# Where the pre-added weight tiles of a two-layer trunk are loaded from, and when they are rounded

## The chip, the cores and the metric

The kernel runs on one core of a Trainium2 chip. The metric is the device time of one execution in microseconds (us); lower is better. Three runs of the kernel before took 2234.64, 2239.62 and 2239.37 us, so its median is 2239.37 us.

## The reference, cut to what matters

The program computes two layers of a trunk on 256 tokens of width 2048, in fp32. Each layer has two halves:

```
h = rms_norm(x, pre_mix_norm);  mix = two kinds of attention over h @ w_in
x = x + rms_norm(mix @ w_o, post_mix_norm)
h = rms_norm(x, pre_ffn_norm)
x = x + rms_norm((silu(h @ w_gate) * (h @ w_up)) @ w_down, post_ffn_norm)
```

`w_gate` and `w_up` are 2048 x 5632, `w_down` is 5632 x 2048. All weights are read once. The change touches the second half of a layer alone: the gate and up products with the `silu` between them, called the gate stage here, and the product with `w_down`, called the down stage.

## The kernel before, in words

**Products.** TensorE (PE) works in fp32r. To keep fp32 accuracy each operand is split into a rounded part `hi` (or `jh`, `sh`, `Th`) and the rest `lo` (`jl`, `sl`, `Tl`), and one product becomes three matmuls: hi*hi, hi*lo, lo*hi (`product`, L730). Each matmul has 128 x 128 weights loaded and 512 columns streamed.

**Weights.** All weights lie in DRAM in the order of use, as 784 tiles of 128 x 1024 floats (512 KB). `fetch` (L149) issues the loads: a tile goes into one of four `raw` buffers by a DMA on SyncE's queue (SP, L159). `feed` (L195) splits a loaded tile: ScalarE (ACT) rounds it into `hi` (L205), and VectorE (DVE) subtracts to get `lo` (L207). There are six `hi` and six `lo` buffers. A product asks for its tile and for the four that follow (`LOOKAHEAD`).

**Gate stage.** It runs over eleven chunks of 512 columns (L854). In each chunk eight pairs `kp` of 128-row blocks are summed; a pair has one tile of `w_gate` and one of `w_up`. Both halves of the tokens meet both tiles, so an ordinary pair is eight products of 128 x 128 x 512, 24 matmuls (`eight`, L837). For some pairs the 2 x 2 block product is done with seven products instead, 21 matmuls (`seven`, L847, and `seven_products`, L750). These pairs, called sevens here, are listed in `SEVEN` (in chunk 0 in `FIRST_SEVEN`), those of the down stage in `DOWN_SEVEN`; there a pair is two neighbouring column tiles of `w_down`, summed over 22 pairs, once for each half of the columns.

**Sums for a seven.** It needs sums of weight blocks. One of them is made by the DMA engines: `summed` (L164) loads the up tile into a buffer `T` by a plain DMA on SP (L167), and a second DMA, on GpSimd's queue (POOL, L168), adds the first half of the gate tile onto it. The second must wait until the first has landed. There are three `T` buffers in the gate stage and two in the down stage. `summed` is called `EARLY` tiles ahead of the fetch. The rest is done by `mixed_weights` (L172): ACT rounds `T` and DVE subtracts (L181, L182), DVE makes three more sums (L186 to L188), overwriting the gate tile in its `raw` buffer, and two more roundings and differences give `Th` and `Tl`, first of 512 columns from `T`, then of 1024 from `raw`, called the last rounding and the last difference here. The token side needs sums too: `pair_sums` and `token_sums` (L830, L737) make them on DVE once a layer for each pair in `SEVEN`; in chunk 0 this is spread by `FORM_AT`, which says ahead of which step which pair's sums are made.

**End of a chunk.** Four banks `p1`, `p6`, `p7`, `q5` that the sevens share are folded into the results (`shared_part`, L767), then DVE adds the four results, ACT applies Silu, and DVE multiplies (L878 to L883). The activations are transposed on PE and copied by ACT into `act` (`flip`, L885). `flip` is started with a delay of `DEFER_ACT` ticks; a tick (`tick`) is counted once every six matmuls or so as products are emitted, so `DEFER_ACT` = 5 puts the transposes in the second pair of the following chunk.

**Order.** A planner orders the instructions of each engine when the program is built, from their priorities and its own estimate of when their inputs are ready; `issue_after` forbids it to put an instruction ahead of a named one. On the chip each engine and each DMA queue runs its instructions strictly in that order, and one that waits holds up all behind it.

Of the kernel before, what the change touches and what calls it, by code (L numbers as in the profile page):

```python
# [2 lines left out]

# [9 lines left out]
AF = mybir.ActivationFunctionType  # L13
# [11 lines left out]
FF = 5632  # L25
CW = 512
# [2 lines left out]
LOOKAHEAD = 4  # L29
PACE = 2  # L30
DEFER = 8
DEFER_ACT = 5
URGENT = 50
TAIL = 3
KP_O = (4, 5, 6, 7, 0, 1, 2, 3)
SEVEN = (2, 4, 5, 6)
FIRST_SEVEN = (4, 6)
FIRST_ORDER = (0, 1, 3, 2, 4, 5, 6, 7)
FORM_AT = {1: 4, 3: 6, 4: 5, 5: 2}
DOWN_SEVEN = (2, 5, 8, 11, 14, 17)  # L40

WARM = 13
LEVEL = 232
EARLY = 4


def lambda_init(layer):
# [58 lines left out]
def kernel(  # L106
# [15 lines left out]
    nc = tc.nc  # L122
# [23 lines left out]
    raws, loads = [], []  # L146
# [15 lines left out]
    sums = {}  # L162

    def summed(i):  # L164

        sums[i] = mix_pool[0].tile([P, 2, CW], F32, tag="T", bufs=mix_pool[1], name=f"T{i}")
        loads.append(nc.sync.dma_start(sums[i], stream[i]))  # L167
        nc.gpsimd.dma_start(sums[i][:, 0, :], stream[i - 1][:, 0, :], accum_op=ALU.add)  # L168

    mix_pool = [None, 0, 0]  # L170

    def mixed_weights(i):  # L172

        g, u = raws[i - 1], raws[i]
        hi = wpool.tile([P, 2, CW], F32R, tag="hi", bufs=6, name=f"hi{i}")
        lo = wpool.tile([P, 2, CW], F32R, tag="lo", bufs=6, name=f"lo{i}")
        th = mix_pool[0].tile([P, 3, CW], F32R, tag="Th", bufs=2, name=f"Th{i}")
        tl = mix_pool[0].tile([P, 3, CW], F32R, tag="Tl", bufs=2, name=f"Tl{i}")

        def split(h, l, w):  # L180
            nc.scalar.activation(h, w, AF.Copy)  # L181
            nc.vector.tensor_tensor(out=l, in0=w, in1=h.bitcast(F32), op=ALU.subtract)  # L182

        split(hi, lo, u)
        t2 = u[:, 1, :]
        nc.vector.tensor_tensor(out=t2, in0=u[:, 0, :], in1=t2, op=ALU.add)  # L186
        nc.vector.tensor_tensor(out=g[:, 0, :], in0=t2, in1=g[:, 0, :], op=ALU.subtract)
        nc.vector.tensor_tensor(out=g[:, 1, :], in0=t2, in1=g[:, 1, :], op=ALU.add)  # L188
        split(th[:, 2, :], tl[:, 2, :], t2)
        split(th[:, 0:2, :], tl[:, 0:2, :], g)  # L190
        t1, b22 = ((hi[:, k, :], lo[:, k, :]) for k in range(2))
        t3, t4, t2 = ((th[:, k, :], tl[:, k, :]) for k in range(3))
        return {"b22": b22, "t1": t1, "t2": t2, "t3": t3, "t4": t4}

    def feed(upto):  # L195
        fetch(upto)
        while fed[0] < min(upto, len(stream)):
            i = fed[0]
# [3 lines left out]
                fed[0] += 1  # L202
                continue
            hi = wpool.tile([P, 2, CW], F32R, tag="hi", bufs=6, name=f"hi{i}")
            nc.scalar.activation(hi, raw, AF.Copy)  # L205
            lo = wpool.tile([P, 2, CW], F32R, tag="lo", bufs=6, name=f"lo{i}")
            nc.vector.tensor_tensor(out=lo, in0=raw, in1=hi.bitcast(F32), op=ALU.subtract)  # L207
            ready[i] = (hi, lo)
# [145 lines left out]
    def start(gen, n=1):  # L354
        running.append([clock[0] + n, gen])
# [421 lines left out]
    for l in range(L):  # L777
# [73 lines left out]
            a11, a12, a22 = (e[:, 0, 0:P], e[:, 1, 0:P]), (o[:, 0, 0:P], o[:, 1, 0:P]), (o[:, 0, P:S], o[:, 1, P:S])  # L851
            seven_products(banks, extra, forms[kp], a11, a12, a22, hi, lo, m, first, last)

        for c in range(FF // CW):  # L854
            banks = four_banks(c % 2, [f"c{q}_{l}_{c}" for q in ("11", "12", "21", "22")])
            mine = FIRST_SEVEN if c == 0 else SEVEN
            order = FIRST_ORDER if c == 0 else tuple(range(KT // 2))
# [21 lines left out]
            for t, u in ((0, w[1]), (1, w[3])):  # L879
                nc.vector.tensor_tensor(out=sg[t], in0=banks[2 * t], in1=sg[t], op=ALU.add)  # L880
                nc.scalar.activation(sg[t], sg[t], AF.Silu, scale=rs[t][:, 0:1])
                nc.vector.tensor_tensor(out=u, in0=banks[2 * t + 1], in1=u, op=ALU.add)
                nc.vector.scalar_tensor_tensor(out=sg[t], in0=u, scalar=rs[t][:, 0:1], in1=sg[t], op0=ALU.mult, op1=ALU.mult)  # L883

            def flip(sg=sg, at=at, c=c):  # L885
# [5 lines left out]
                    yield 1  # L891

            start(flip(), DEFER_ACT)
        gu.release()
        mix_pool[:] = new_x_pool(f"sums{l}"), 2, plan[l]["down"][3, FF // P // 2 - 1] + 1
        dn = tc.alloc_tile_pool(name=f"dn{l}", bufs=4, reuse_waits="tile")
# [146 lines left out]
```

## Time and profile before

| | us |
|---|---|
| median of 3 runs | 2239.37 |
| lowest and highest | 2234.64, 2239.62 |
| the profiled execution | 2239.96 |
| its span, first to last instruction | 2237.9 |
| busy in the span: PE, DVE, ACT, POOL | 2200.9, 1789.1, 1309.5, 132.0 |
| gate stage, layer 0 and layer 1, about | 412 to 882, 1526 to 1996 |

A row of the profile names the engine, the line of the kernel and the tiles as out<-in. "SPq" is the queue of SyncE, and the DMAs of L168 stand under POOL. PE's matmuls overlap: each is shown with about 0.39 us, but the next starts 0.23 us after it, so PE can be shown as busy while it is waiting, and starts are to be compared, not durations. DVE's steps overlap a little in the same way.

### The profile page before, as it was taken

To read this page: it belongs to the slowest core of one execution; us is meant where nothing else is said; L and a number is where in the kernel's file an instruction comes from. 1 tells how busy PE (TensorE), PEld (TensorE's weight loads), DVE (VectorE), ACT (ScalarE), POOL (GpSimd) and SP (SyncE) were. 2 spreads that over 40 slices of the span, in tenths; PEclk is the share of its full clock that TensorE was granted. 3 is DMA by queue.
4 is the path that set the end of the run, shared out by engine and by line. 5 is a ranking of instruction groups with operands and counts; after the bars stand their busy time and mean duration, and the time that the engine had idled before them with its cause. 6 is when DMAs were issued, how large, how long until landed. Compare 5 with 4: busy or idle time off the path is not lost.

```text
span 2237.9 us, 28440 instructions
## 1 busy us (share of the span) xinstructions
PE 2200.9 (98%) x10057; PEld 1802.2 (81%) x10057; DVE 1789.1 (80%) x2531; ACT 1309.5 (59%) x1937; POOL 132.0 (6%) x184
## 2 busy tenths in 40 slices
PE   9999999999999999999999999999999999999998
PEld 7888888777887888788878888887777887878886
DVE  6666555899988999989776665558999999998897
ACT  6545554665655656656565455546665566566664
POOL 1100000000000000000010000000000000000000
PEclk9999999999999999999999999999999999999999
DMA  8555455576776676766555544556677677666673
GB/s 290 189 167 164 160 190 183 186 223 209 226 242 199 212 251 190 228 214 205 193 184 171 168 162 160 188 186 192 206 218 237 218 222 234 221 203 222 203 232 132
DMA packets 133326, 452.05 MB, mean 202 GB/s; under 512 B 15296, under 2 KB 15808, under 8 KB 132672
## 3 DMA queue, kind: packets, MB, share of 16 engines
q1 hardware_dynamic: 117488, 421.91, 55.2%
q0 software_dynamic: 15552, 28.32, 7.6%
q8 instruction: 79, 1.29, 0.2%
q14 instruction: 63, 0.52, 0.1%
q10 hardware_dynamic: 144, 0.02, 0.0%
HBM read 448.09 MB, written 2.10 MB: 201 GB/s over the span
## 4 chain that ended last, share of the span: by engine, by line
PE 71%; DVE 13%; DMA 6%; issue 4%; ACT 4%; POOL 0%; DVEq 0%; ACTq 0%; SPq 0%; POOLq 0%
PE in L380 7%; PE in L382 7%; PE in L381 7%; DMA raw<-in_weights_in_turn_dram 5%; PE c L733 5%; PE c L734 5%; PE c L735 5%; PE dn L938 5%; PE dn L936 5%; PE dn L935 4%; DVE lo L207 3%; DVE Tl L182 2%; PE o L382 2%; PE o L381 2%; PE o L380 2%
## 5 line engine op out<-in xcount | busy, mean ns | idle before, releaser
L207 DVE TENSOR_TENSOR lo<-raw,hi 128x1024 fp32r<-128x1024 f32 x675 | 824.1, 1225 | 311.4 <-ACT hi L205 307.3
L205 ACT ACTIVATE hi<-raw 128x1024 fp32r<-128x1024 f32 x675 | 709.4, 1057 | 510.9 <-DMA raw<-in_weights_in_turn_dram 178.4
L733 PE MATMUL c<-hi,xF 128*128 128x512 f32 x820 | 321.0, 395 | 2.4 <-DVE w L774 1.3
L735 PE MATMUL c<-hi,xF 128*128 128x512 f32 x820 | 318.8, 391 | 0.0
L734 PE MATMUL c<-lo,xF 128*128 128x512 f32 x820 | 318.7, 389 | 0.0
L168 POOL DMA_DIRECT2D T<-in_weights_in_turn_dram x108 | 94.1, 871 | 1754.1 <-DMA T<-in_weights_in_turn_dram 821.8
L733 PEld LDWEIGHTS c<-hi,xF 128*128 128x128 f32 x820 | 154.0, 188 | 35.3 <-DVE w L774 2.5
L936 PE MATMUL dn<-lo,jh 128*128 128x512 f32 x464 | 180.8, 390 | 0.0
L935 PE MATMUL dn<-hi,jh 128*128 128x512 f32 x464 | 180.7, 389 | 0.0
L735 PEld LDWEIGHTS c<-hi,xF 128*128 128x128 f32 x820 | 153.9, 188 | 32.3
L734 PEld LDWEIGHTS c<-lo,xF 128*128 128x128 f32 x820 | 154.1, 188 | 30.9
L380 PE MATMUL in<-hi,xI 128*128 128x512 f32 x384 | 154.0, 401 | 0.2 <-ACT xI L321 0.2
L380 PE MATMUL in<-hi,xT 128*128 128x512 f32 x384 | 153.4, 400 | 0.2 <-ACT xT L616 0.2
L382 PE MATMUL in<-hi,xI 128*128 128x512 f32 x384 | 150.2, 391 | 0.3 <-DVE xI L326 0.3
L381 PE MATMUL in<-lo,xI 128*128 128x512 f32 x384 | 149.9, 390 | 0.5 <-DVE lo L207 0.5
L381 PE MATMUL in<-lo,xT 128*128 128x512 f32 x384 | 149.8, 390 | 0.5 <-DVE lo L207 0.5
L382 PE MATMUL in<-hi,xT 128*128 128x512 f32 x384 | 150.2, 391 | 0.0
L938 PE MATMUL dn<-hi,jl 128*128 128x512 f32 x464 | 143.3, 390 | 0.0
L182 DVE TENSOR_TENSOR Tl<-raw,Th 128x1024 fp32r<-128x1024 f32 x108 | 131.5, 1217 | 8.7 <-ACT Th L181 8.7
L181 ACT ACTIVATE Th<-raw 128x1024 fp32r<-128x1024 f32 x108 | 113.8, 1053 | 37.9 <-DVE raw L188 37.8
L182 DVE TENSOR_TENSOR lo<-T,hi 128x1024 fp32r<-128x1024 f32 x108 | 131.4, 1216 | 4.4 <-ACT hi L181 4.4
L181 ACT ACTIVATE Th<-T 128x512 fp32r<-128x512 f32 x108 | 67.9, 629 | 112.1 <-DVE T L186 96.3
(298 smaller groups left out, 4077.9 us busy)
## 6 DMA issues: line engine op xcount, KB each, us to landing
raw<-in_weights_in_turn_dram SPq DMA_DIRECT2D x675, 512.0 KB, 4.3
T<-in_weights_in_turn_dram SPq DMA_DIRECT2D x108, 512.0 KB, 4.4
T<-in_weights_in_turn_dram POOLq DMA_DIRECT2D x108, 256.0 KB, 6.5
xr<-in_x_columns_dram SPq DMA_DIRECT2D x8, 256.0 KB, 6.1
x<-in_x_dram SPq DMA_DIRECT2D x4, 512.0 KB, 9.2
gpost_mix<-in_post_mix_norm_dram SPq DMA_DIRECT2D x2, 1024.0 KB, 6.0
gpost_ffn<-in_post_ffn_norm_dram SPq DMA_DIRECT2D x2, 1024.0 KB, 8.1
out_dram<-x SPq DMA_DIRECT2D x8, 256.0 KB, 2.8
```

Source lines behind the costliest of these rows:

```text
L182: nc.vector.tensor_tensor(out=l, in0=w, in1=h.bitcast(F32), op=ALU.subtract)
L205: nc.scalar.activation(hi, raw, AF.Copy)
L207: nc.vector.tensor_tensor(out=lo, in0=raw, in1=hi.bitcast(F32), op=ALU.subtract)
L380: nc.tensor.matmul(a, sh, hi[:, kk, :], start=first and kk == 0, stop=False)
L381: nc.tensor.matmul(a, sh, lo[:, kk, :], start=False, stop=False)
L382: nc.tensor.matmul(a, sl, hi[:, kk, :], start=False, stop=last and kk == 1)
L733: nc.tensor.matmul(a, sh, hi, start=first, stop=False)
L734: nc.tensor.matmul(a, sh, lo, start=False, stop=False)
L735: nc.tensor.matmul(a, sl, hi, start=False, stop=last)
L935: nc.tensor.matmul(accs[c, t], sh, hi[:, kk, :], start=first, stop=False)
L936: nc.tensor.matmul(accs[c, t], sh, lo[:, kk, :], start=False, stop=False)
L938: nc.tensor.matmul(accs[c, t], sl, hi[:, kk, :], start=False, stop=last)
```

## The change

Six things are changed together.

- The plain load of `T` goes to GpSimd's queue, just ahead of the adding DMA of the same tile, and is no longer in the list `loads` that `load_gain` is ordered behind.
- `mixed_weights` notes its last rounding in `turns`; the rounding of an ordinary tile `i` may not be put ahead of the last rounding of any seven with `j <= i - 2` (`after_sums`).
- `DEFER_ACT` becomes 7, so the transposes come two ticks later.
- `EARLY` becomes 6.
- The sevens move: in the gate stage from pairs 2, 4, 5, 6 to 2, 3, 5, 6, in chunk 0 from 4, 6 to 5, 6, in the down stage from 2, 5, ... 17 to 3, 6, ... 18. Their number is the same, and so is the number of matmuls. `FORM_AT` follows.
- The two multiplications at the end of a chunk are written behind both pairs of sums. (The body of the loop over chunks becomes a function.)

```
-DEFER_ACT = 5
+DEFER_ACT = 7
...
-SEVEN = (2, 4, 5, 6)
-FIRST_SEVEN = (4, 6)
+SEVEN = (2, 3, 5, 6)
+FIRST_SEVEN = (5, 6)
 FIRST_ORDER = (0, 1, 3, 2, 4, 5, 6, 7)
-FORM_AT = {1: 4, 3: 6, 4: 5, 5: 2}
-DOWN_SEVEN = (2, 5, 8, 11, 14, 17)
+FORM_AT = {1: 5, 2: 6, 4: 2, 5: 3}
+DOWN_SEVEN = (3, 6, 9, 12, 15, 18)
...
-EARLY = 4
+EARLY = 6
...
         sums[i] = mix_pool[0].tile([P, 2, CW], F32, tag="T", bufs=mix_pool[1], name=f"T{i}")
-        loads.append(nc.sync.dma_start(sums[i], stream[i]))
+        nc.gpsimd.dma_start(sums[i], stream[i])
         nc.gpsimd.dma_start(sums[i][:, 0, :], stream[i - 1][:, 0, :], accum_op=ALU.add)
...
+    turns = []
+
+    def after_sums(i):
+
+        done = [ins for j, ins in turns if j <= i - 2]
+        return tc.issue_after(done[-1]) if done else nullcontext()
...
         def split(h, l, w):
-            nc.scalar.activation(h, w, AF.Copy)
+            rounded = nc.scalar.activation(h, w, AF.Copy)
             nc.vector.tensor_tensor(out=l, in0=w, in1=h.bitcast(F32), op=ALU.subtract)
+            return rounded
...
-        split(th[:, 0:2, :], tl[:, 0:2, :], g)
+        turns.append((i, split(th[:, 0:2, :], tl[:, 0:2, :], g).ins))
...
-            nc.scalar.activation(hi, raw, AF.Copy)
+            with after_sums(i):
+                nc.scalar.activation(hi, raw, AF.Copy)
...
                 nc.vector.tensor_tensor(out=u, in0=banks[2 * t + 1], in1=u, op=ALU.add)
+            for t, u in ((0, w[1]), (1, w[3])):
                 nc.vector.scalar_tensor_tensor(out=sg[t], in0=u, scalar=rs[t][:, 0:1], in1=sg[t], op0=ALU.mult, op1=ALU.mult)
```

More of the change, by code (lines that the diff above doesn't have):

```diff
@@ L1 @@
 import math
-from contextlib import ExitStack
+from contextlib import ExitStack, nullcontext
 import concourse.bass as bass
@@ L852, in seven, with chunk @@
             seven_products(banks, extra, forms[kp], a11, a12, a22, hi, lo, m, first, last)
-        for c in range(FF // CW):
+        def chunk(c):
             banks = four_banks(c % 2, [f"c{q}_{l}_{c}" for q in ("11", "12", "21", "22")])
@@ L893 @@
             start(flip(), DEFER_ACT)
+        for c in range(FF // CW):
+            chunk(c)
         gu.release()
```

## The prediction

> **What bounds the kernel now.** I read the page first, then who waited for whom on PE, then single chunks by time.
>
> ```profile
> PE 2200.9 (98%) x10057; PEld 1802.2 (81%) x10057; DVE 1789.1 (80%) x2531; ACT 1309.5 (59%) x1937; POOL 132.0 (6%) x184
> ```
>
> ```profile
> PE p L733 <- ACT Th L181: 6.5, 11, 1.5
> PE p L734 <- DVE Tl L182: 5.1, 9, 0.9
> PE p_d L733 <- ACT Th L181: 4.9, 2, 2.5
> ...
> PE actT_ps L889 <- DVE w L883: 2.1, 4, 0.9
> ```
>
> TensorE is the bound, and no matmul is added or removed, so only its pauses can be won. The second fence (us in total, times, longest) is most of them in the stages that the change touches: 6.5 + 5.1 + 4.9 + 2.1 = 18.6 us, most of it for the last sums of a seven. Each is counted from the modelled end of a matmul, so by starts a pause is a little longer. The starts of the first product with `Th` in pair 6 show how much:
>
> ```profile
> 529.12 0.39 PE L733 MATMUL p<-Th,sh 128*128 128x512 f32 x1
> ...
> 789.47 0.39 PE L733 MATMUL p<-Th,sh 128*128 128x512 f32 x1
> 831.26 0.39 PE L733 MATMUL p<-Th,sh 128*128 128x512 f32 x1
> 873.10 0.39 PE L733 MATMUL p<-Th,sh 128*128 128x512 f32 x1
> ...
> 1643.66 0.39 PE L733 MATMUL p<-Th,sh 128*128 128x512 f32 x1
> 1984.60 0.39 PE L733 MATMUL p<-Th,sh 128*128 128x512 f32 x1
> ```
>
> From 789.47 to 831.26 a chunk takes 41.79 us without a pause: 180 matmuls and 8 short transposes, 0.23 us a matmul. From chunk 2 (529.12) to chunk 10 (873.10) eight chunks take 343.98 us, 9.7 over 8 x 41.79 = 334.3; in layer 1, 340.94, 6.6 over. So 16.3 us are lost in these sixteen chunks. A part is not waiting but a slow clock:
>
> ```profile
> 789.47:831.26 41.79, 41.79 (x190) 34.50 (x188) 39.19 (x47) 25.30 (x29) 3.48 (x4) 1.00 0.73 229
> 704.95:708.36 3.41, 3.41 (x9) 2.65 (x8) 2.96 (x4) 0.34 (x1) 0.61 (x1) 0.50 1.08 333
> 899.51:902.92 3.41, 3.41 (x10) 2.64 (x9) 3.41 (x5) 2.41 (x3) 0.00 (x0) 0.50 0.89 281
> ```
>
> In these windows the granted clock (third number from the end) falls to 0.50 for 3.41 us, right behind the longest pauses of layer 0 (1.5 and 0.9 above, and 2.35 below), which costs 1.7 us each time. The Trainium skill, "TensorE: Matmul & The Clock Gate", "What's actually happening", says that TensorE drops to half clock after an idle window of about 3.4 us. The trace is stricter: shorter pauses did it here.
>
> The first row also shows DVE (the fourth number with a bracket is ACT, the third DVE) busy for 39.19 of 41.79 us. It has 2.6 us of play in a chunk, and its order decides when the last sums of a seven are there:
>
> ```profile
> 825.45 0.68 DVE L186 TENSOR_TENSOR T<-T 128x512 f32<-128x512 f32 x1
> 826.05 1.22 DVE L207 TENSOR_TENSOR lo<-raw,hi 128x1024 fp32r<-128x1024 f32 x1
> ...
> 829.00 1.21 DVE L207 TENSOR_TENSOR lo<-raw,hi 128x1024 fp32r<-128x1024 f32 x1
> 830.13 1.22 DVE L182 TENSOR_TENSOR Tl<-raw,Th 128x1024 fp32r<-128x1024 f32 x1
> ```
>
> Steps follow each other after 0.60 us (512 columns) or 1.14 us (1024). The last difference of pair 6 ends at 831.35. The product that uses it is the one after 831.26, so it starts at 831.49: 0.14 us of margin in a chunk without a pause. Any DMA that is late breaks it, as in this piece of the chain that ended last, where PE was waiting:
>
> ```profile
> 694.57 6.25 DMA raw<-in_weights_in_turn_dram
> ...
> 703.14 1.23 DVE Tl L182
> ```
>
> An ordinary load takes 6.25 us; its rounding stands ahead of the last rounding of pair 6 on ACT, so that the difference that PE needs comes at 703.14.
>
> **The change, part by part.** *Ordering roundings behind the sums.* In the old order the two differences shown at 826.05 and 829.00, of tiles for pair 7 and the next chunk, stand ahead of the last difference of pair 6. In the new order they stand behind it, and so do their roundings on ACT. That takes 2 x 1.14 = 2.3 us off its time: the margin goes from 0.14 to about 2.4 us. What is pushed back is late next: the difference of the first up tile of the following chunk. PE takes this one only after pair 7 (24 matmuls), so it is covered; uncovered it would cost its 1.14.
>
> *Sevens at 2, 3, 5, 6.* Three in a row become two and two, so a late seven no longer pushes the next two; pair 3 now needs its sums one pair earlier, with the steps of pair 2 just ahead. In the new order its last difference comes two long and four short DVE steps after that of pair 2 (4.7 us), and PE's products with it 21 matmuls after (4.8 us), so it costs 0 in a chunk that runs level. In the first two chunks, where DVE comes late from the end of the attention half, it may cost up to 2 us a layer. I keep these chunks at a gain of 1 us, between a loss of 4 and a gain of 5: of the waits above 13.7 us belong to the gate stage, and with some 0.16 more for each of 24 by starts they are 17.6, of which the sixteen chunks hold 16.3 - 1.7 = 14.6; 3 are left for the first chunks, and 2 for smaller groups.
>
> *T through POOL.* Three things.
>
> ```profile
> T<-in_weights_in_turn_dram SPq DMA_DIRECT2D x108, 512.0 KB, 4.4
> ```
>
> ```profile
> SPq L167 <- DVE Tl L182: 319.5, 98, 8.4
> ```
>
> SP sheds 108 issues and 319.5 us in which it stood at L167 for a free buffer with later `raw` loads behind it. The `raw` loads wait for their own buffers anyway, so I count no gain. POOL gets 108 issues, 0.87 us each by those that it has:
>
> ```profile
> L168 POOL DMA_DIRECT2D T<-in_weights_in_turn_dram x108: 853/866/1011, 418.1 to 2171.2; - x108
> ...
> DMA to landing us min/median/max: 3.6/6.5/8.6
> ```
>
> That is 94 us on an engine that is busy for 132 of 2238; nothing else is queued on it in these stages. What matters is the chain buffer free, plain DMA, adding DMA, rounding. Today:
>
> ```profile
> 807.32 0.33 SPq L167 DMA_DIRECT2D T<-in_weights_in_turn_dram  x1
> ...
> 821.62 1.04 ACT L181 ACTIVATE hi<-T 128x1024 fp32r<-128x1024 f32 x1
> ```
>
> The tightest is `T` of pair 6, whose buffer pair 2 frees: 14.3 us from issue to use, of which the two DMAs take 4.4 + 6.5 = 10.9 by their medians. In the new order eight long and eight short DVE steps lie between (13.9 us); less a rounding of 1.05 there is room for 12.9. The plain load by POOL appears in no row. Below it is bounded by SP's own, 4.4; above by POOL's own copies of half the size, 6.5 median, twice that (13) if bytes decide. I take 5.3, near SP's: the adding DMA must also fetch what it adds to. Chain 0.1 + 5.3 + 6.5 = 11.9, inside 12.9; cost 0. The Trainium skill, "SBUF — State Buffer", "SBUF: two separate sides", warns that a DMA from GpSimd's queue starves while DVE holds the shared port in a two-port mode, and advises SyncE's or ScalarE's queue. With DVE busy for 94% of the chunk, POOL's 108 issues took 853 to 1011 ns, so the trace shows no starving here.
>
> At the start of a stage POOL issues the second plain load only after the first adding DMA:
>
> ```profile
> 413.11 0.90 SPq L167 DMA_DIRECT2D T<-in_weights_in_turn_dram  x2
> ...
> 431.27 1.04 ACT L181 ACTIVATE hi<-T 128x1024 fp32r<-128x1024 f32 x1
> ```
>
> Now both plain loads are issued at once. Then the second `T` is complete at about 413.1 + 5.3 + 0.9 + 5.3 + 6.5 = 431.1 by the values above; its seven keeps its place in chunk 0, and its rounding began at 431.3. Cost 0, at worst 1.
>
> *EARLY 6.* With three buffers the free buffer decides, not the call: 0.
>
> *DEFER_ACT 7.* The transposes come twelve matmuls later. The four waits for L883 (2.1 us) go; ACT copies their result later, ahead of the rounding for pair 3, which has time until DVE is through with pair 2. Gain 2, already within the chunk sums and those of chunks 0 and 1.
>
> *Down stage from pair 3.* Its first `T` can load only when the gate stage's last matmul is done:
>
> ```profile
> 881.50 0.81 SPq L167 DMA_DIRECT2D T<-in_weights_in_turn_dram  x2
> ...
> 899.02 0.82 PE L733 MATMUL p_d<-Th,sh 128*128 128x512 f32 x2 [2.35 <-ACT Th L181]
> ```
>
> One pair later gives 24 matmuls, 5.5 us, more than the pause of 2.4 to 2.5 in each layer (4.9 together). The first chain may be 1 us longer on POOL and is still covered. The slow clock at 899.51 goes too (1.7). Gain 4.9 + 1.7 = 6.6, less 0.5 for what may be left.
>
> *The multiplications behind the sums:* two DVE steps change places, 0.
>
> **Sum.** Of 16.3 us in the sixteen chunks I take off 13; the other 3 stay in chunks 2 to 4, where DVE with 2.6 us of play is still catching up. 13 + 6 + 1 = 20. The profiled execution took 2239.96 us (span 2237.9), 0.6 over the median: 2240 - 20 = 2220, and 2219 for the median.
>
> **Rivals.** *DVE stays the limit (2234).* The pauses may come from too little play altogether, and a new order then only moves them: DVE's work a chunk is the same 39.2 us, and new waits for `raw` buffers could eat the 2.6. Then only the down stage's 6 us are won: 2234. For it speaks that DVE is busy for 94% of a chunk; against it that with the same work the chunk from 831.26 to 873.10 takes 41.84 too.
>
> *The software queue is too slow (2282).* If the plain load takes 13 us, the chain is 19.6; 6.7 over the room, 2.6 of which DVE's play takes. Every chunk would take 41.8 + 4.1 = 45.9 instead of the 42.8 that they take on average: 16 x 3.1 = 50, less the 7 won elsewhere, about 2282. It decides from about 10 us for the plain load: there chunks take 42.9, as now. Against it: the slowest of POOL's 108 DMAs took 8.6. Longer issues would do the same from 16.5 us for the chain, 2.3 more for each of the two, where the rows spread over 0.16.
>
> *All pauses go (2211).* 16.3 + 6.6 + 5 = 28 is the end below.
>
> **Chances.** The forecast, 2211 to 2230, 0.66 with what lies below it. DVE stays the limit, 2230 to 2240, 0.19, a third of it below 2232.7. Slower by the queue or by starving 0.15. A difference of 0.3% (6.7 us) is about what a measurement of this kernel can tell from none. Faster by more: 0.66 + 0.06 = 0.72; within: 0.13; slower: 0.15. The range runs from 2211 to 2238, the first two cases; the forecast's own is 2211 to 2230.
>
> **What would show it.** In the changed kernel the waits of PE for `Th` and `Tl` fall from 16.5 us to under 5, those for L883 and of `p_d` nearly vanish, no window at half clock stands at the start of the down stage, and chunks 3 to 10 take 41.8 us each. POOL's issues number 216 at 0.87 us, and the plain ones land in 4.4 to 6.5. The forecast is wrong if ACT waits for `T` in pair 6, if chunks stay over 42.5, or if `Th` of pair 3 becomes what PE waits for.

## The result and the profile after

The changed kernel is slower. Four runs took 2299.37 to 2308.01 us, median 2305.32; the kernel before has a median of 2238.4 over the three runs above and one more. The ratio is 1.0298, with a 95% interval of 1.0274 to 1.0322. The forecast was 2219.

The profiled execution took 2299.37 us (span 2297.7), 59.4 more than that of before. First the page's line of the engines, then PE's waits in the stages of the change (us in total, times, longest). In the changed kernel the lines above 200 have moved down by some eight: L741 to L743 are the three matmuls of a product, L779 to L782 the fold, L187 and L188 the rounding and the difference of a seven, L213 and L215 those of an ordinary tile.

```profile
PE 2216.7 (96%) x10057; PEld 1795.4 (78%) x10057; DVE 1791.6 (78%) x2531; ACT 1304.9 (57%) x1937; POOL 192.0 (8%) x292
```

```profile
PE p L742 <- DVE Tl L188: 18.2, 22, 1.3
PE c L741 <- DVE w L782: 16.0, 14, 1.4
PE c L741 <- DVE w L779: 13.1, 11, 1.8
PE p L741 <- ACT Th L187: 8.3, 9, 2.0
PE dn L949 <- DVE jl L924: 3.3, 2, 1.7
PE c L741 <- DVE w L780: 2.1, 3, 0.8
...
PE p_d L742 <- DVE Tl L188: 1.7, 1, 1.7
```

PE's work is the same and the span is longer. The waits that the change was to remove grew (`Tl` from 5.1 to 18.2 us, `Th` from 6.5 to 8.3), and the largest is one that was small before: 31.2 us for `w`, the fold of the shared banks, in three groups. Before, it was 2.0 us in two:

```profile
PE c L733 <- DVE w L774: 1.3, 2, 0.7
...
PE c L733 <- DVE w L772: 0.7, 2, 0.5
```

The next chunk's products write into the banks that the fold reads, so PE cannot begin the chunk before it. By the starts of PE (a chunk is dated by the first product with `Th` of its pair 6, as in the prediction) the time stands here, in us, after minus before:

| | layer 0 | layer 1 |
|---|---|---|
| start of the gate stage to chunk 2 | +5.4 | +2.6 |
| chunks 2 to 10 | +25.3 | +26.9 |
| from chunk 10 to the next gate stage, or the end | -0.2 | -0.5 |

So nearly all of the loss lies between chunk 2 and chunk 10, called the level chunks here. Their windows, one row a layer, of before and of after (span, then busy PE, PEld, DVE, ACT, POOL):

```profile
529.12:873.10 343.98, 338.51 (x1506) 276.76 (x1504) 315.69 (x371) 204.25 (x235) 26.96 (x31) 1.00 0.71 219
1643.66:1984.60 340.94, 336.61 (x1506) 275.58 (x1504) 315.71 (x372) 204.19 (x235) 26.99 (x31) 1.00 0.70 221
```

```profile
534.83:904.11 369.28, 344.20 (x1505) 274.09 (x1504) 314.26 (x369) 199.69 (x232) 42.23 (x59) 1.00 0.66 202
1677.07:2044.88 367.81, 344.17 (x1506) 274.43 (x1504) 313.82 (x369) 199.53 (x232) 42.20 (x59) 1.00 0.66 202
```

DVE's work is the same to 2 us in 315. What grew is the time in which DVE does nothing: 343.98 - 315.69 = 28.3 us before, 369.28 - 314.26 = 55.0 after, or 3.5 and 6.9 us a chunk. The chain of work shows what sets the pace. In the first of these windows, by line, of before and then of after:

```profile
by line: PE c L733 15.1%; PE c L735 15.1%; PE c L734 15.1%; DMA raw<-in_weights_in_turn_dram 7.3%; issue 6.7%; DVE lo L207 5.4%; PE p L734 4.4%; DVE Tl L182 4.2%; PE p L735 4.2%; PE p L733 4.0%; DVE lo L182 3.4%; DVE T L186 2.1%; DVE raw L1
```

```profile
by line: DMA raw<-in_weights_in_turn_dram 23.0%; DVE lo L215 12.3%; issue 10.6%; DVE Tl L188 8.8%; DVE lo L188 6.5%; ACT hi L213 5.8%; DVE raw L194 3.9%; PE c L741 3.5%; DVE T L193 3.5%; PE c L743 3.5%; PE c L742 3.4%; DVE w L890 2.4%; DVE 
```

Before, the matmuls shown are 58% of the chain. After, they are 10%; 23% are loads of `raw` tiles, and DVE's rows make up 37%. One turn of it, from the chain of after between 794 and 846 us (start, us, what):

```profile
794.67 1.15 DVE lo L215
...
795.83 7.16 DMA raw<-in_weights_in_turn_dram
...
803.10 1.07 ACT hi L213
...
804.19 0.58 DVE lo L215
...
808.36 1.13 DVE Tl L188
...
812.03 1.15 DVE lo L215
...
813.19 5.68 DMA raw<-in_weights_in_turn_dram
...
822.72 0.61 DVE w L779
...
840.96 1.15 DVE lo L215
842.12 5.87 DMA raw<-in_weights_in_turn_dram
```

There is no matmul in this stretch of the chain. A difference on DVE frees a `raw` buffer (794.67), SP starts the next load at once (795.83), ACT rounds it (803.10), DVE goes on by its difference (804.19) to the last difference of a seven (808.36) and to the one that frees the next buffer (812.03); the next load (813.19) stands in front of the fold (822.72). The turn closes at 842.12, 46.3 us after 795.83, and 7.16 + 5.68 = 12.8 us of it are two loads for which the chain waits. DVE and PE by time at the end of that chunk:

```profile
814.22 2.35 DVE L215 TENSOR_TENSOR lo<-raw,hi 128x1024 fp32r<-128x1024 f32 x2
820.07 1.23 DVE L215 TENSOR_TENSOR lo<-raw,hi 128x1024 fp32r<-128x1024 f32 x1 [3.50 <-ACT hi L213]
821.50 1.22 DVE L215 TENSOR_TENSOR lo<-raw,hi 128x1024 fp32r<-128x1024 f32 x1 [0.20 <-ACT hi L213]
...
825.70 0.68 DVE L782 TENSOR_TENSOR w<-q,w 128x512 f32<-128x512 f32 x1
```

```profile
826.44 0.50 PE L741 MATMUL c<-hi,xF 128*128 128x512 f32 x1 [1.37 <-DVE w L782]
```

DVE stands for 3.50 us in front of the difference of the next chunk's first up tile. The fold (L779 to L782) is behind that difference and behind one more, of the gate tile of pair 1. It has nothing to wait for itself, and is through at 826.4; PE has waited for it for the last 1.37 us.

### The profile page after: what moved, and what is told of

It reads as the page before. It is cut to its first block, busy times and chain, and to the rows that moved or that the text cites. A ratio compares the mean times of both kernels' runs of the same rounds, so it can differ in the third digit from the quotient of the medians.

```text
span 2297.7 us, 28437 instructions
## 1 busy us (share of the span) xinstructions
PE 2216.7 (96%) x10057; PEld 1795.4 (78%) x10057; DVE 1791.6 (78%) x2531; ACT 1304.9 (57%) x1937; POOL 192.0 (8%) x292
## 4 chain that ended last, share of the span: by engine, by line
PE 55%; DVE 22%; DMA 12%; issue 6%; ACT 5%; POOL 0%; SPq 0%; DVEq 0%; ACTq 0%; POOLq 0%
DMA raw<-in_weights_in_turn_dram 12%; PE in L388 7%; PE in L390 7%; PE in L389 7%; DVE lo L215 6%; PE dn L949 4%; PE dn L947 4%; PE dn L946 4%; DVE Tl L188 4%; ACT hi L213 3%; DVE lo L188 3%; PE o L390 2%; PE o L388 2%; PE o L389 2%; DVE T L193 2%
## 5 line engine op out<-in xcount | busy, mean ns | idle before, releaser
L215 DVE TENSOR_TENSOR lo<-raw,hi 128x1024 fp32r<-128x1024 f32 x675 | 821.2, 1225 | 377.7 <-ACT hi L213 373.7
L213 ACT ACTIVATE hi<-raw 128x1024 fp32r<-128x1024 f32 x675 | 708.7, 1056 | 522.0 <-DMA raw<-in_weights_in_turn_dram 261.9
L741 PE MATMUL c<-hi,xF 128*128 128x512 f32 x820 | 327.2, 400 | 32.3 <-DVE w L782 16.0
L743 PE MATMUL c<-hi,xF 128*128 128x512 f32 x820 | 320.2, 392 | 0.0
L741 PEld LDWEIGHTS c<-hi,xF 128*128 128x128 f32 x820 | 153.9, 188 | 80.3 <-DVE w L782 23.0
L743 PEld LDWEIGHTS c<-hi,xF 128*128 128x128 f32 x820 | 154.2, 188 | 32.5
L167 POOL DMA_DIRECT2D T<-in_weights_in_turn_dram x108 | 65.6, 608 | 1273.2 <-DVE Tl L188 547.5
L187 ACT ACTIVATE Th<-T 128x512 fp32r<-128x512 f32 x108 | 68.0, 630 | 174.8 <-DVE T L193 174.8
L187 ACT ACTIVATE Th<-raw 128x1024 fp32r<-128x1024 f32 x108 | 113.9, 1055 | 62.3 <-DVE raw L195 62.3
L188 DVE TENSOR_TENSOR Tl<-raw,Th 128x1024 fp32r<-128x1024 f32 x108 | 131.6, 1218 | 8.0 <-ACT Th L187 8.0
L168 POOL DMA_DIRECT2D T<-in_weights_in_turn_dram x108 | 93.9, 869 | 491.6 <-DMA T<-in_weights_in_turn_dram 491.6
```

Of the source, the lines that this page charges most:

```text
L741: nc.tensor.matmul(a, sh, hi, start=first, stop=False)
L743: nc.tensor.matmul(a, sl, hi, start=False, stop=last)
```

## The experiments

Each run is timed against the kernel before on the same chip (its medians there were 2234.6 to 2238.4, so times of different sets are to be compared by their ratios); the ratio has its 95% interval. "8 chunks" is the time from chunk 2 to chunk 10 in layer 0 and layer 1 by PE's starts (before: 344.0 and 340.9).

| run | us | ratio | 8 chunks |
|---|---|---|---|
| the changed kernel | 2305.3 | 1.0298 (1.0274 to 1.0322) | 369.3, 367.8 |
| e1 new places alone | 2269.6 | 1.0143 (1.0121 to 1.0165) | 350.9, 349.5 |
| e2 roundings behind sums alone | 2238.3 | 1.0014 (1.0004 to 1.0023) | 341.1, 341.7 |
| e3 queue alone | 2259.2 | 1.0093 (1.0065 to 1.0122) | 350.1, 346.3 |
| e4 changed, old places | 2260.2 | 1.0104 (1.0085 to 1.0122) | 345.8, 349.0 |
| e5 down stage and transposes | 2232.1 | 0.9986 (0.9976 to 0.9995) | 338.0, 341.1 |
| e6 changed, T on SP | 2272.0 | 1.0158 (1.0137 to 1.0179) | 348.0, 348.2 |
| e7 new places, five raw buffers | 2254.5 | 1.0083 (1.0067 to 1.0099) | 338.9, 338.9 |
| e8 changed, fold ahead | 2253.5 | 1.0078 (1.0053 to 1.0102) | 340.4, 342.6 |
| e9 new places, fold ahead | 2260.3 | 1.0113 (1.0099 to 1.0127) | 349.3, 346.4 |
| e10 old places, fold ahead | 2238.5 | 1.0017 (1.0008 to 1.0026) | 337.8, 339.5 |
| e11 e8 with T on SP | 2257.2 | 1.0101 (1.0085 to 1.0116) | 344.7, 339.7 |
| e12 changed, no roundings behind sums | 2291.8 | 1.0245 (1.0223 to 1.0266) | 362.0, 363.6 |
| e13 queue, pair 4 alone | 2235.0 | 1.0002 (0.9991 to 1.0014) | 341.1, 342.4 |
| e14 queue, pair 2 alone | 2249.1 | 1.0055 (1.0041 to 1.0068) | 343.9, 345.4 |
| e15 changed, five raw buffers | 2250.9 | 1.0069 (1.0055 to 1.0082) | 340.3, 340.4 |
| e16 five hi buffers alone | 2295.8 | 1.0268 (1.0249 to 1.0287) | 355.6, 353.0 |
| e17 transposes alone | 2236.8 | 0.9998 (0.9988 to 1.0007) | 341.4, 341.1 |
| e18 down stage alone | 2234.6 | 0.9988 (0.9977 to 0.9998) | 339.2, 341.9 |

The first theory was that the new places of the sevens cause the loss (P). Its rivals were the ordering of the roundings (S) and the queue (Q). The theory was mended twice, after e9 and after e13 and e14.

### One part alone

**e1**, the kernel before with

```
-SEVEN = (2, 4, 5, 6)
-FIRST_SEVEN = (4, 6)
+SEVEN = (2, 3, 5, 6)
+FIRST_SEVEN = (5, 6)
...
-FORM_AT = {1: 4, 3: 6, 4: 5, 5: 2}
+FORM_AT = {1: 5, 2: 6, 4: 2, 5: 3}
```

> The kernel before with the new places of the sevens in the gate stage alone (2, 3, 5, 6; in chunk 0: 5, 6) and the table that follows them. Theory P, places: two sevens in a row hold two of the four raw buffers until their last differences, so the loads of the next chunk's tiles are issued some 4 us later, and DVE stands in its fixed order in front of them, ahead of the fold of the shared banks that PE waits for. Then this edit alone gives most of the loss: 2270 to 2310 us, chunks of 44 to 46 us, and PE waits for the fold (w) at the starts of chunks. Theory S, sums: the loss comes from the roundings that are kept behind the sums of a seven; then this edit alone gives 2235 to 2245. Theory Q, queue: the loss comes from the T loads that POOL issues; then also 2235 to 2245.

Measured 2269.6, just under the 2270 to 2310 of P, with chunks of 43.8 us on average: by the ratios it is about half of the loss, not most of it. PE's wait for the fold, and the chain from chunk 2 to chunk 10 of layer 0:

```profile
PE c L733 <- DVE w L774: 16.5, 14, 1.4
```

```profile
by line: DMA raw<-in_weights_in_turn_dram 24.4%; issue 13.7%; DVE lo L207 13.2%; DVE Tl L182 12.2%; DVE lo L182 7.8%; ACT hi L205 5.5%; DVE raw L187 4.7%; DVE T L186 4.0%; DVE w L883 3.0%; DVE w L882 3.0%; DVE raw L188 2.3%; DVE w L771 1.3%
```

The new places alone turn the chunks into the same loop: the shown part of the chain holds no matmul, and the wait for the fold is there. Of the 30.2 us between the two spans, 15.5 are lost in the sixteen level chunks, 4.6 from the start of the gate stage to chunk 2, and 8.3 behind chunk 10, nearly all in the down stages. The loads show why the level chunks lose. Here is when loads of `raw` tiles are issued and land, in us after PE's first product with `Th` of pair 6, each the median of seven chunks of layer 0:

| tile | before | e1 | after | e15 |
|---|---|---|---|---|
| gate, pair 5 | -24.5, -21.1 | -20.0, -16.6 | -20.8, -17.0 | -32.2, -27.7 |
| gate, pair 7 | -21.6, -16.3 | -15.2, -9.9 | -16.0, -9.9 | -18.4, -11.8 |
| gate, pair 0 of the next chunk | -8.0, -3.9 | -4.7, -1.5 | -4.7, -0.2 | -13.0, -7.8 |
| up, pair 0 of the next chunk | -5.7, -1.5 | -1.0, 4.0 | -1.0, 5.6 | -4.0, -0.6 |
| gate, pair 1 of the next chunk | -3.9, 2.4 | 0.1, 5.8 | 0.1, 7.0 | -2.3, 3.8 |

With the old places the load for pair 5 was issued when the difference of pair 3's gate tile, an ordinary one, had freed its buffer. Pair 3 is now a seven and holds its gate tile to its last difference; the first buffer to come free is that of pair 2, after its own last difference, and the load goes out 4.5 us later. The gate tile of pair 7 is then 6.4 us later, the planner puts its difference behind the sums of pair 6, just ahead of the last difference, and with it go the loads for the next chunk, by 3.3 to 4.7 us.

**e2**, the kernel before with `after_sums` (the two blocks of the diff that make `turns`, and the `with` around the rounding).

> The kernel before with the roundings kept behind the sums of a seven, and nothing else. Theory P: the last difference of pair 6 is earlier by two long steps of DVE, as the prediction had it, and no buffer is held longer: 2222 to 2236 us. Theory S: 2270 to 2310 us, and SP waits for the last differences of sevens (Tl) for over 500 us. Theory Q: 2222 to 2236.

Measured 2238.3, ratio 1.0014: no gain, and outside the 2222 to 2236 that P gave. PE's waits and the chain:

```profile
PE c L741 <- DVE w L782: 6.2, 6, 2.6
...
PE p L741 <- ACT Th L187: 2.1, 3, 0.9
```

```profile
by line: issue 14.6%; DMA raw<-in_weights_in_turn_dram 13.0%; DVE Tl L188 11.4%; DVE lo L215 10.8%; DVE lo L188 8.9%; DVE raw L194 6.1%; DVE T L193 5.5%; ACT hi L213 3.8%; ACT Th L187 3.7%; PE c L743 3.0%; PE c L741 3.0%; PE c L742 3.0%; DV
```

The wait for `Th` fell from 6.5 to 2.1 us, as the margin said. But the fold is now waited for 6.2 us (2.0 before), and the chain is already that of DVE and the loads. The time just moved.

**e3**, the kernel before with

```
-        loads.append(nc.sync.dma_start(sums[i], stream[i]))
+        nc.gpsimd.dma_start(sums[i], stream[i])
```

> The kernel before with the plain load of T on GpSimd's queue and nothing else (still called four tiles ahead, sevens at 2, 4, 5, 6). Theory Q: a T load that is needed a chunk later goes out together with raw loads that are needed at once and shares their bandwidth; raw loads then land after 7 to 8 us in place of 3.4 to 5.8, and the time is 2260 us or more. Theories P and S: within 7 us of the kernel before, 2231 to 2245.

Measured 2259.2, ratio 1.0093: 0.8 us under the 2260 of theory Q, where P and S had both said no change. So the loss has two causes. Of the 22.5 us between the two spans 11.5 are lost in the level chunks. There the orders of ACT and DVE are those of the kernel before but for a few steps near chunks 3 and 4, and the `raw` loads are issued at nearly the same points of a chunk (-8.3 and -6.0 for the two tiles of pair 0 of the next chunk). They land later, though by less than Q said. (Ahead of chunk 2 and in the down stages, with 10.3 us, the planner chose other orders too, so that this part is not the queue's alone.) Issue to landing of the `raw` loads from chunk 2 to chunk 10 in layer 0, of before and of e3, and PE's waits in e3:

```profile
DMA to landing us min/median/max: 3.2/5.2/8.2
```

```profile
DMA to landing us min/median/max: 3.1/5.6/8.3
```

```profile
PE p L734 <- DVE Tl L182: 10.2, 15, 1.0
PE p L733 <- ACT Th L181: 10.0, 11, 1.5
```

The gate tile of pair 0 now takes 6.14 us in place of 4.07 (medians of seven chunks). Its rounding stands ahead of the last rounding of pair 6 on ACT, and PE waits 20.2 us for the last sums in place of 11.6, and 7.5 for the fold in place of 2.0. The moved loads of `T` land later as well, in the same window of before and of e3:

```profile
DMA to landing us min/median/max: 3.3/4.6/7.2
```

```profile
DMA to landing us min/median/max: 3.4/6.3/8.5
```

But that is not what costs: ACT waits 7.9 us in all for a `T` that is not complete, and 8.1 before. The Trainium skill, "DMA: Bandwidth & Descriptors", "Issuing engines are not separate DMA queues", says that DMAs started by different engines run on the same sixteen DMA engines and interleave, so that a second queue saves only the time of issuing. The landings agree: the same loads, issued at the same points, land later beside a second queue. (Which load does it is another matter, e13 and e14.)

**e5, e17, e18**, the kernel before with both or one of

```
-DEFER_ACT = 5
+DEFER_ACT = 7
...
-DOWN_SEVEN = (2, 5, 8, 11, 14, 17)
+DOWN_SEVEN = (3, 6, 9, 12, 15, 18)
```

> The kernel before with the sevens of the down stage at 3, 6, ... 18 and the transposes two ticks later, nothing else. The prediction gave these parts 6.6 - 0.5 us for the down stage (its pauses of 4.9 us for the last sums and the half clock behind one of them) and 2 us for the transposes: 2227 to 2230 us. Theory W (the wait moves): PE then waits for the sums of the first seven or for the split activations (jl) instead, as in the changed kernel, where the two stages came out level: 2233 to 2240.

> The kernel before with the transposes two ticks later and nothing else. The prediction: the four waits of PE for the products of the activations (2.1 us at L883) go, 2237 us. If the gain of the run with both parts (3.5 us) is all from here: 2231 to 2234. If it delays the rounding for pair 2 or 3 on ACT: 2238 or more.

> The kernel before with the sevens of the down stage at 3, 6, ... 18 and nothing else. The prediction gave 6.1 us: 2230 to 2233 by the shared runs of the kernel before. Theory W (the first pause shrinks and the second seven waits in its place, as in the run with both parts, where the profile shows 2.4 us won over the two down stages): 2233 to 2237.

Measured: both 0.9986 (2232.1, between the two ranges), transposes alone 0.9998, down stage alone 0.9988 (2234.6, as W said). The transposes are worth nothing that can be seen, although PE's wait for them falls from 2.1 to 0.6 us. The down stage is worth 2.7 us by the ratio, 0.4 to 5.1 by its interval. PE's waits, for the transposes in e17 and for the down stage's first sums in e18, which are still there, for `Tl` now:

```profile
PE actT_ps L889 <- DVE w L883: 0.6, 1, 0.6
```

```profile
PE p_d L734 <- DVE Tl L182: 2.4, 2, 1.2
```

The second seven is late next: the first two of the stage stand 17.1 and 18.9 us apart in the two layers, 15.64 between later ones. A stretch at half clock is still there too: in e18 the granted clock is 0.50 for 3.41 us from 2011.9, at the first seven of the down stage of layer 1.

### One part taken out of the changed kernel

**e4**, the old `SEVEN`, `FIRST_SEVEN` and `FORM_AT`; **e6**, the plain load of `T` on SP; **e12**, no `with after_sums(i)`.

> The changed kernel with the sevens of the gate stage back at 2, 4, 5, 6 (chunk 0: 4, 6), all its other parts kept. Theory P: the loss goes, 2215 to 2235 us, chunks of 41.8 to 42.5 us. Theories S and Q: it stays at 2280 us or more.

> The changed kernel with the plain load of T back on SyncE's queue, all else kept. The places alone cost 34 us and the queue alone 23. Theory A (the two causes add up): 2268 to 2278 us. Theory B (with the new places the loads of T are early enough, and the queue costs nothing there): 2295 to 2308.

> The changed kernel without the roundings kept behind the sums; DVE's order around the end of a chunk stays as it is by the planner's own choice. Theory P: the chunks stay as slow (45 to 46 us), 2290 to 2308. Theory S (the held roundings cost something with these places): under 2285.

By the ratios the old places give back 43 us, the old queue 31, the old order of roundings 12, and none of the three gives back all. e4 missed both what P said (2215 to 2235) and what S and Q said (2280 or more): what is left, 1.0104, is about what the queue alone costs (1.0093). e6 came as theory A said, by adding up. e12 came as P said. It shows that the slow chunks need no `after_sums`; with the new places and the new queue that part makes eight chunks 4 to 7 us longer.

### Buffers and the fold

**e7** is e1, and **e15** the changed kernel, each with five `raw` buffers; **e16** is the kernel before with the `hi` line alone.

```
-  tag="raw", bufs=4
+  tag="raw", bufs=5
...
-  tag="hi", bufs=6
+  tag="hi", bufs=5
```

> The new places alone (the run that took 2270 us), with five raw buffers in place of four; the room comes from one of the six hi buffers. Theory P (loads of the next chunk's tiles are late because sevens in a row hold the buffers): raw loads go out earlier, the waits of PE for the fold (w, 16.5 us at L774) fall below 5 us, and the time to 2235 to 2250. Theory O (the new places simply ask DVE for too much in a row, whatever the buffers): the waits and the time stay, 2262 us or more. Five hi buffers can cost something of their own, so a time between the two is read by the waits.

> The changed kernel with five raw buffers in place of four and five hi buffers in place of six. Theory P (the raw loads are late because the sevens in their new places hold the buffers): PE's waits for w fall from 31 us to under 8, chunks 2 to 10 take 338 to 346 us a layer in place of 369 and 368; with what five hi buffers cost elsewhere, 2250 to 2270 us. If the queue alone made them late: chunks of 355 us or more, 2285 or more.

> The kernel before with five hi buffers in place of six and nothing else: the price of the room that the runs with five raw buffers took. By those runs' stages outside the chunks of the gate stage it costs 7 to 14 us there: 2240 to 2252. If it is dearer, the gain by the fifth raw buffer was larger than the times show.

PE's waits in e7, those in e15, and the chain of e15 from chunk 2 to chunk 10:

```profile
PE c L733 <- DVE w L774: 3.7, 2, 2.0
...
PE p L734 <- DVE Tl L182: 2.2, 2, 1.1
```

```profile
PE c L741 <- DVE w L782: 2.0, 1, 2.0
...
PE p L742 <- DVE Tl L188: 0.8, 2, 0.4
```

```profile
by line: PE c L743 23.5%; PE c L741 23.5%; PE c L742 23.5%; PE p L741 7.3%; PE p L742 7.2%; PE p L743 6.5%; PE q L743 2.1%; PE q L741 2.1%; PE q L742 2.1%; PE actT_ps L898 2.1%; ACT Th L187 0.3%; ACTq L213 0.0%; issue 0.0%
```

With a fifth buffer the waits for the fold and for `Tl` nearly vanish, the chain is matmuls from end to end, and eight chunks take 340.3 and 340.4 us in place of 369.3 and 367.8, with the queue and all else of the changed kernel in place. e15 met all that P said of it; e7 met the wait and missed the time (2254.5, not 2235 to 2250). The gate tile of pair 0 is issued 8.3 us earlier than after (-13.0).

But the planner's order changed with the buffer. The first step of the fold now stands ahead of the difference for pair 1, and in e7 the difference of pair 7's gate tile is ahead of the sums of pair 6 again. So the buffer and the order that comes with it are not separated by these runs. e8 below gets the same eight chunks (340.4 and 342.6) out of the changed kernel by an order alone, with four buffers. For the buffer speaks e9, whose fold is ahead as well and which still takes 349.3 and 346.4 us where e7 takes 338.9.

e16 is no clean price of the room: it cost 60 us, not 7 to 14, and here too the order changed. The planner put the difference of pair 7's gate tile behind the sums of pair 6, as with the new places; the loads for pair 0 of the next chunk go out at -3.6 and -0.6 us, later than with the new places; and PE waits 25.8 us for the activations ahead of the transposes. What five `hi` buffers cost by themselves is not known, and the fifth `raw` buffer may be worth more than e7 and e15 show.

**e8** is the changed kernel with the differences of later tiles held behind the fold:

```
+            with tc.issue_after(folds[-1]) if folds else nullcontext():
                 nc.vector.tensor_tensor(out=lo, in0=raw, in1=hi.bitcast(F32), op=ALU.subtract)
...
-        nc.vector.tensor_tensor(out=w[3], in0=q5, in1=w[2], op=ALU.subtract)
+        folds.append(nc.vector.tensor_tensor(out=w[3], in0=q5, in1=w[2], op=ALU.subtract).ins)
```

**e9** has that, the new places, the down stage from pair 3 and the later transposes, on the kernel before; **e10** the same with the old places; **e11** is e8 with `T` on SP.

> The changed kernel with one order more: the differences of tiles that are fed after the fold of the shared banks (the gate tile of pair 1 of the next chunk and what follows) may not stand ahead of the fold on DVE. The differences of pair 0 stay ahead of it. Theory F (the fold is late because it stands in DVE's order behind differences whose tiles are still being loaded): the fold comes 1.4 us earlier or more, PE's waits for w fall from 31 us to 10 to 18, and the time by 12 to 25 us, to 2280 to 2294. Rival (PE then waits as long for the differences that were pushed back): within 5 us of 2305.

> The kernel before with the new places, the fold ahead of the differences fed after it, the down stage from pair 3 and the later transposes; T stays on SyncE's queue and no rounding is held behind sums. Theory F (the new places lose only by the late fold): chunks 2 to 10 take 336 to 342 us a layer (before: 344 and 341), the first chunks are 2 to 4 us shorter than before, as with the new places alone: 2220 to 2232 us, faster than both kernels. Rival (late raw loads cost elsewhere once the fold is out of the way, at the first sums of a seven): 2238 us or more.

> As the run with new places and the fold ahead, with the old places. Theory F: in the old places the loads are early enough that the fold is hardly ever late (waits for w of 2 us), so the order changes little against the same kernel without it (2232): 2226 to 2236 us. Rival (the order is a gain of its own wherever the sevens are): under 2222.

> The changed kernel with the fold ahead (2253) and the plain load of T back on SyncE's queue. If the queue costs what it cost alone (23 us): 2228 to 2236. If most of its cost came by way of the late fold: 2244 to 2254.

e8 gave 52 us by the medians, 49 by the ratios, where 12 to 25 were expected: the difference for pair 1 no longer stands ahead of the fold, and a few steps of pairs 2 and 3 change places with it. The chain of e8 from chunk 2 to chunk 10, and the wait that is left:

```profile
by line: PE c L743 16.9%; PE c L744 16.8%; PE c L745 16.8%; DMA raw<-in_weights_in_turn_dram 5.6%; issue 5.1%; PE p L744 4.9%; PE p L745 4.7%; DVE lo L217 4.5%; PE p L743 4.5%; DVE Tl L189 4.0%; DVE lo L189 3.0%; DVE T L194 2.0%; PE q L743 
```

```profile
PE p L744 <- DVE Tl L189: 12.9, 21, 1.2
```

Matmuls lead the chain again, and eight chunks take 340.4 and 342.6 us, against 344.0 and 340.9 in the kernel before: the loss in the level chunks is gone. The loads for pair 0 of the next chunk still go out late (-5.6 and -1.9 us, with -8.0 and -5.7 before). So late loads alone do not cost this time; in the changed kernel they do, where the fold stands behind their differences in DVE's order. What e8 still loses lies ahead of chunk 2 (10.3 us in the two layers) and in the down stages (5.6).

A part of the gain over the expected may come from the loads. In the changed kernel the `T` load for pair 5 goes out 0.8 us ahead of the load of the next chunk's first up tile, which then takes 6.7 us; in e8 it goes out 0.4 us behind it, and that tile takes 3.9 (medians of seven chunks). No run tries this by itself. With the fold ahead, the queue costs nothing (e8 1.0078, e11 1.0101, which missed both of its ranges); with it behind, 31 us (e6 and the changed kernel).

But e9 missed: the fold is no longer waited for, and the time is 2260 all the same. Its waits:

```profile
PE p L736 <- DVE Tl L183: 20.5, 24, 2.1
...
PE c L735 <- DVE w L776: 0.7, 1, 0.7
```

PE waits for the last sums of a seven in its place, 24 times, and eight chunks take 349.3 and 346.4 us. So in e9 the fold was the place where the late tiles showed, and with it out of the way they show at the next one. In e8 and e11 they do not: there the level chunks lose nothing, and the 17 and 23 us over the kernel before lie elsewhere. These two have the ordering of the roundings, `EARLY` 6 and the other order of the multiplications, which e9 has not; which of these makes the difference was not tried. e10, with the old places, missed its 2226 to 2236. PE never waits for the fold in it, and it shows no gain by the order itself.

### Which load of the queue

**e13** and **e14** move the plain load of one pair of the gate stage alone to POOL, on the kernel before:

```
+        if 128 <= i % 392 < 304 and (i % 392 - 128) % 16 // 2 == 4:
+            nc.gpsimd.dma_start(sums[i], stream[i])
+        else:
+            loads.append(nc.sync.dma_start(sums[i], stream[i]))
```

(e14 has 2 in place of 4.)

> The kernel before with the plain load of T on GpSimd's queue for pair 4 of a chunk of the gate stage alone (22 loads of 108); all others stay on SyncE's queue, and the orders of ACT and DVE are those of the kernel before. This load is issued 2 us ahead of the raw load of the next chunk's first tile. Theory H (two queues share the DMA engines, so a raw load that is needed soon lands later when a T load that is needed late is under way in the other queue): this one load brings 8 to 20 of the 23 us, 2243 to 2255 us, and that raw load lands about 2 us later than before (4.07 us after its issue there). Theory G (the software queue costs by its issues or its own slowness, each load alike): a fifth of 23 us, 2236 to 2242.

> The same for pair 2 alone (20 loads). This load is issued 2 to 3 us ahead of the raw load of the up tile of pair 7, which is needed late. Theory H: 2232 to 2240 us, within 4 us of the kernel before. Theory G: a fifth of 23 us, 2236 to 2242, as for pair 4.

Both theories fell: each run lies outside both of its ranges. The load beside the urgent tile (pair 4) costs nothing, that of pair 2 costs 12 us by the ratio, over half of the 21 of e3. In e14 ACT and DVE have exactly the orders of the kernel before, so these 12 us are the queue's alone. (In e13 the orders differ at a few places up to chunk 3.) PE's wait for `Tl`, in e13 and then in e14:

```profile
PE p L737 <- DVE Tl L185: 6.0, 11, 0.9
```

```profile
PE p L737 <- DVE Tl L185: 12.1, 16, 0.9
```

The next chunk's first gate tile lands 3.9 us ahead of PE's pair 6 before, 2.9 in e13, 2.2 in e14, 2.1 in e3. That fits e13 and e14, but e3 loses 8 us more than e14 with the same landing, so it is not the whole. In e14 the delay is handed on along SP's queue, by medians of seven chunks: the tile of pair 7 beside the moved load takes 4.42 us in place of 3.27, the `T` load behind it 6.83 in place of 5.11, the gate tile behind that 5.84 in place of 4.07. Why the delay grows on the way, and why pair 4's load hands on less, the runs do not show.

No version is clearly faster than both kernels. The best, e5, is at 0.9986, inside the 0.3% that a measurement can tell from none.

## Why the prediction was wrong

**What bounds the kernel now.** Right for the kernel before by its chain, but it left out how near the other loop was. DVE's 2.6 us of play were treated as DVE's alone. They are the play of a loop of DVE, `raw` buffers, loads and ACT: what DVE stands waiting for a late load comes off them too, and once they are gone the chunk takes DVE's 39.3 us plus what it stands idle, 6.9 us in the changed kernel. (One sum is off by 0.1: 13.7 and 24 times 0.16 are 17.5, not 17.6. Nothing hangs on it.)

**Sevens at 2, 3, 5, 6: "costs 0 in a chunk that runs level".** This is the step that failed most: 34 us alone, 15.5 of them in these chunks, where it said 0, and 4.6 in the first chunks, where it said a gain of 1. The working compared DVE's steps with PE's matmuls and did not ask what a seven in place of an ordinary pair does to the four `raw` buffers. The gate tile of pair 3 is held to its last difference, and the loads behind it go out 3.3 to 6.4 us later, more than the play. Nor did it ask what stands behind the differences of those tiles in DVE's order: the fold, and in e9 the last sums. Both belong to the cause in the level chunks, as e8 has the late loads and loses nothing there. That the held buffers make the loads late is read from what released each load; that a fifth one cures it is shown only together with the order that came with it.

**T through POOL: "The `raw` loads wait for their own buffers anyway, so I count no gain", cost 0.** Right about the issues, wrong about the landings: 23.5 us alone. What was priced was the chain of `T` itself, and that held: ACT waits 8.4 us for `T` in the changed kernel, 8.1 before. POOL's rows of after (busy us and mean ns of one, then what it waited for) stand first below; then us from issue to landing, minimum, median and maximum, of the plain loads in chunks 2 to 10 of layer 0; then the same for the `raw` loads:

```profile
L168 POOL DMA_DIRECT2D T<-in_weights_in_turn_dram x108 | 93.9, 869 | 491.6 <-DMA T<-in_weights_in_turn_dram 491.6
L167 POOL DMA_DIRECT2D T<-in_weights_in_turn_dram x108 | 65.6, 608 | 1273.2 <-DVE Tl L188 547.5 <-ACT junk_ffn L352 280.7 <-PE xT_ps L326 276.8
```

```profile
DMA to landing us min/median/max: 3.5/3.7/8.2
```

```profile
DMA to landing us min/median/max: 3.2/5.9/8.4
```

The issue takes 0.61 us, not 0.87. The median of 3.7 hides two groups: 15 of these 29 plain loads took 3.5 to 3.7 us and the others 5.5 to 8.2, on average 5.2, close to the 5.3 taken. The rival "The software queue is too slow" is refuted, as none came near 10 us, and no starving shows. What it cost was the other queue: the `raw` loads' median went from 5.2 to 5.6 us in e3 and to 5.9 here. Nothing in the prediction priced the loads beside the moved one.

**Ordering roundings behind the sums: margin from 0.14 to 2.4 us, 13 us with the rest.** The margin came (the wait for `Th` fell to 2.1 us in e2), the gain did not. That PE takes the pushed-back tile "only after pair 7 (24 matmuls), so it is covered" leaves out the fold behind it in DVE's order, which PE needs for the next chunk's banks. The fold was named in no step.

**EARLY 6 and the order of the multiplications: 0.** Not tried alone. **DEFER_ACT 7: 2 us** within the sums: 0 (e17). **Down stage: 6.1 us:** right in sign, 2.7 measured (e18); the pause at the first sums halved and the second seven became late. In the changed kernel little of it is left (0.7 us in the two layers): `jl` and `Tl` are waited for at the stage's start (3.3 and 1.7 us).

**The parts together.** By the ratios new places, queue, roundings, and down stage with transposes add up to 2.36% alone, and the whole is 2.98%. The other 0.6%, 14 us, is what the parts do to each other, or belongs to `EARLY` and the multiplications, which no run tries alone.

**Rivals.** "DVE stays the limit" named the mechanism ("new waits for `raw` buffers could eat the 2.6") and priced it at no loss, 2234. It stopped at the point where the play is gone. Worked on from there with the delay that e1 shows for the gate tile of pair 0, 3.3 us less 2.6 of play, it gives 16 x 0.7 = 11 us of loss, an estimate after the fact; e1 lost 15.5 in those chunks. So the mechanism stood in the text, as a rival, without the step that would have sized it.

## What to carry to other kernels

Where an engine in a fixed order has a few per cent of play, list what frees each load buffer before and after a change, and when: a tile that is held for a few steps more delays every load behind it, and the place where that shows can be a quite different wait. When a load moves to a second DMA queue, price the loads beside it too: in e3 both the loads that stayed and those that moved landed later (medians 5.2 to 5.6 and 4.6 to 6.3 us). Look at what stands behind a late tile in an engine's fixed order, as one step moved ahead can be worth as much as a buffer. And read the chain of work for the stage, not only the waits of the busiest engine: here it had changed from matmuls to loads and differences while PE still showed 96% busy.

## What the runs showed of the hardware

Plain loads of 512 KB from GpSimd's queue took 0.61 us to issue on average in the changed kernel, against 0.87 for the adding DMA. They landed neither reliably sooner nor later than the same size from SyncE's queue: in two groups of 3.5 to 3.7 and 5.5 to 8.2 us in the changed kernel, and with a median of 6.3 us in e3, where SyncE's queue had taken 4.6 for the same loads before. Moving a single load per chunk to the other queue (20 loads, e14), with the orders of ACT and DVE unchanged, made a load two places further down SyncE's queue take 1.8 us longer from issue to landing. The granted clock fell to 0.50 for 3.41 us behind pauses of PE of 2.35 us, and of 1.5 and 0.9 us in a row (the kernel before).
